# A bidirectional encoder layer: rsqrt of the input norm folded into retention, sums of squares taken tile by tile, the backward sweep in other PSUM banks

## The chip, the cores and the metric

The kernel runs on one core of a Trainium2 chip. The metric is the device time of one execution in microseconds; before the change it is 2090.89 us, the median of three runs from 2088.53 to 2091.76. TensorE makes the matmuls and transposes, VectorE (DVE), ScalarE (ACT) and GpSimd (POOL) work on elements, and SyncE (SP) issues every DMA of this kernel, in the order of its queue.

## The reference, cut to what matters

Two sequences, 512 and 1024 tokens of width 1024, pass one layer with the same weights: a token mixer (four heads of retention beside a gated MLP), cross-attention to a memory of 256 rows, and a SwiGLU. Each of the three has an RMS norm ahead of it and another behind it. The change touches the mixer.

```python
def rms_norm(x, w):
    y = x * rsqrt(mean(x * x, axis=-1) + EPS)
    return y * w
z = rms_norm(x, nw[NORM_PRE_MIX]) @ w_in
q, k, v, g, u, vs = split(z, ...)          # u, vs: the gated MLP; q, k, v, g: retention
q = rotary(q); k = rotary(k) * RET_HEAD_DIM ** -0.5
y = bidir_retention(q, k, v, log_gamma)    # chunks of 128 tokens, states carried both ways
ret_out = silu(g) * group_norm(y) * ret_gn_w
u = gelu(u); vs = layer_norm(gelu(vs), sgu_norm_w)
sgu_out = u * (sgu_w applied within a chunk to vs, + sgu_b)
mixed = concat(ret_out, sgu_out) @ w_out
```

In retention a chunk's scores q k^T are multiplied by a matrix of decays and applied to v; a forward state (sum of decayed k^T v) and a backward state add the other chunks.

## The kernel before, in words

The 1536 tokens are 12 tiles of 128. A float32 product is made of three matmuls (mm3, L149 to L151): both factors are split into a high part, written by ScalarE as fp32r (L135, or L139 with a scale), and the rest, written by VectorE (L136, L140). PSUM has eight banks of 128x512: four with the tag mm, four with the tag sm. A bank is given out again when its last reader is done.

*First stage.* z for u and vs of tiles 0 to 3 is accumulated in all eight banks (L214 to L231) while w_in is loaded. Then x_stats(0, 4) and x_stats(4, 8) (L293) load x tile by tile, ScalarE squares each and sums along the row (L245, L248), and after four tiles VectorE and GpSimd make rs_x = (mean + EPS)^-0.5 (L254, L163, L164). rs_x is then written to rsxd in HBM, transposed (L256), and read back as a row spread over all partitions (L257, rsx_row).

The loop over tiles 4 to 11 (L397) makes u and vs: 48 matmuls of 128x512 a tile (L409) into two mm banks. Between them run parts of generators: a tile's split for the next one (x_tile, L306), make_S, stats (x_stats(8, 12), then mem_stats for the memory's rows), and side, which holds post_uv of finished tiles: Gelu scaled by rs_x of the token, here a partition (L263, L264), layer norm (L266 to L272), two advances later the gating matmuls (L278), two later the transposes (L288) and a store to mixT (L291). make_S takes two tiles of x transposed, multiplies them by rsx_row (L316), forms four sums on GpSimd (L320 to L323), and stores seven left factors Sd (L326).

*z for retention.* q, k, v and g come from a scheme of seven products in place of eight for 2x2 blocks (z_units, 84 of 12 matmuls, mm bank each, L617 to L660): fetch_z loads a left factor (L352), split_z splits it, right_z makes the right factors. The results are added up in SBUF (c11 to c22).

*Retention.* While the z units run, point() (L581), called at most twice a unit, steps every generator in side once and starts a new tile of ret_feed at every second call. ret_tile is one head's chunk: rotary on GpSimd and VectorE (L472 to L477), transposes of q and k (L481, L482) into a bank pa, state products into a bank pb and the scores into pa (L492 to L503), the decays (L505), and in a next step the product with v (L507, L508, L510). ret_back goes over a sequence's chunks from the last to the first: a product with the backward state (L532), group norm, gate (L533 to L547), and one step later finish(): a transpose, a scaled copy (L522 to L524) and a store (L525). All of these banks have the tag sm.

The framework orders each engine's queue ahead of time by its own estimates; an engine works its queue in that order. Later stages (v and k of the memory, projections, attention, SwiGLU) are left as they are.

Of the kernel before, what the change touches and what calls it, by code (L numbers as in the profile page):

```python
# [17 lines left out]
P = 128  # L18
# [64 lines left out]
def encoder_kernel(ctx: ExitStack, tc, x, xTp, xTt, mem, memT, norm_w, w_in, lg, small, sgu_nw, sgu_wT,  # L83
# [23 lines left out]
    def sm():  # L107
        return psp.tile([P, 512], F32, tag="sm", name="sm")
# [89 lines left out]
    DT = [cB[:, 512 + h * P : 640 + h * P] for h in range(4)]  # L198
    swT = cC[:, 0:512]
    snB = cC[:, 512:1024]  # L200
    rsx_row = [sinT[:, 0:512], sinT[:, 512:D], cosT]
# [5 lines left out]
    Sd = {(n, j): dram.tile([P, 512], F32, tag=f"xs{n}_{j}", name=f"xs{n}_{j}") for n in range(1, 8) for j in range(6)}  # L207
    rsxd = dram.tile([NT, P], F32, tag="rsxd", name="rsxd")

    nc.sync.dma_start(sml, small)  # L210
    A.activation(rs_x, neg_half, AF.Copy)
# [20 lines left out]

    ss_x = const([P, NT], "ss_x")

    def squares(src, n, sums, done):

        q = deque()
        for t in n:
            r = raw.next()
            nc.sync.dma_start(r, src[t])  # L240
            q.append((t, r))
            if len(q) > 1:
                yield
                t, r = q.popleft()
                A.activation(r, r, AF.Square, accum_out=sums[:, t : t + 1])  # L245
        yield
        t, r = q.popleft()
        A.activation(r, r, AF.Square, accum_out=sums[:, t : t + 1])  # L248
        done()

    def x_stats(t0, t1):
        def done():
            s = slice(t0, t1)
            V.tensor_scalar_mul(ss_x[:, s], ss_x[:, s], 1.0 / D)  # L254
            rsqrt(rs_x[:, s], ss_x[:, s])
            nc.sync.dma_start(rsxd[t0:t1].rearrange("t p -> p t"), rs_x[:, s])  # L256
            nc.sync.dma_start(rsx_row[t0 // 4], rsxd[t0:t1].rearrange("t p -> (t p)").partition_broadcast(P))  # L257

        return squares(x, range(t0, t1), ss_x, done)

    def post_uv(t, pu, pv):
        u, vg = u_r.next(), vs_r.next()
# [27 lines left out]
        A.activation(m, pt, AF.Copy)  # L290
        nc.sync.dma_start(mixT[t][:, 4:8, :], m.rearrange("p (k t) -> p k t", t=P))  # L291

    for g in (x_stats(0, 4), x_stats(4, 8)):  # L293
        for _ in g:
            pass
    nc.sync.dma_start(swT, sgu_wT)
    nc.sync.dma_start(snB, sgu_nw.partition_broadcast(P))
    raw.slots, raw.i = FA.units[0:2], -1
# [11 lines left out]
        return o  # L310

    def make_S(j, xs):
        for t, r in zip((2 * j, 2 * j + 1), xs):
            r = r.rearrange("p (k t) -> p k t", t=P)
            row = rsx_row[t // 4][:, (t % 4) * P : (t % 4 + 1) * P]
            V.tensor_tensor(r, r, row.unsqueeze(1).broadcast_to([P, KT, P]), op=ALU.mult)  # L316
            yield
        a11, a12, a21, a22 = (r[:, i * 512 : (i + 1) * 512] for r in xs for i in range(2))
        s1, s2, s3, s4 = sums_x
        G.tensor_tensor(s1, a21, a22, op=ALU.add)  # L320
        G.tensor_tensor(s2, s1, a11, op=ALU.subtract)
        G.tensor_tensor(s3, a11, a21, op=ALU.subtract)
        G.tensor_tensor(s4, a12, s2, op=ALU.subtract)  # L323
        yield
        for n, src in ((1, a11), (2, a12), (4, a22), (5, s1), (6, s2), (7, s3), (3, s4)):
            nc.sync.dma_start(Sd[n, j], src)  # L326


# [1 line left out]
    rs_m = const([P, 4], "rs_m")  # L330

    def mem_stats():
        def done():
            V.tensor_scalar_mul(ss_m, ss_m, 1.0 / D)
            rsqrt(rs_m, ss_m)
            nc.sync.dma_start(rsd.rearrange("t p -> p t"), rs_m)

        return squares(mem, range(4), ss_m, done)

# [9 lines left out]
    def fetch_z(i):  # L349
        if i < len(z_units):  # L350
            Sq[i] = S_land.next()
            nc.sync.dma_start(Sq[i], Sd[z_units[i][1:]])  # L352

    def split_z(i):
        if i < len(z_units):
# [36 lines left out]
    for t in range(4):  # L392
        g = post_uv(t, *first[t])
        next(g)
        side.append(g)
    stats = x_stats(8, NT)
    for t in range(4, NT):  # L397
        a = nxt
        pss = [mm(), mm()]
        if t in (5, 8):  # L400
            x_load(0 if t == 5 else 2)
            x_load(1 if t == 5 else 3)
        j = {5: 2, 6: 0, 7: 3, 9: 4, 10: 1, 11: 5}.get(t)
        blocks = iter(()) if j is None else make_S(j, [xs.pop(2 * j), xs.pop(2 * j + 1)])
        for k in range(KT):
            ak = ksl(a, k)
            for x0, x1, st, sp in ((0, 0, True, False), (0, 1, False, False), (1, 0, False, True)):
                for i in range(2):
                    T.matmul(pss[i], lhsT=ak[x0], rhs=W[k][x1][:, i * 512 : i * 512 + 512],  # L409
                             start=st and k == 0, stop=sp and k == KT - 1)  # L410
            if k == 1 and t + 1 < NT:
                nxt = x_tile(t + 1)
            if t == NT - 1 and k % 2 == 0:
                right_z(1, 1, k // 2)
            if k % 2:
                next(blocks, None)
                next(stats, None)
            if k % 4 == 3 or t == 4 and k % 2:
                advance()
        g = post_uv(t, *pss)  # L420
        next(g)
        side.append(g)
        if t == 6:
            stats = mem_stats()
    RX = Part([RX.tiles[0], big("rx1", F32R), RX.tiles[2]])
    T_r.slots = T_r.slots + RX.units[7:9] + RX.units[3:5]
# [4 lines left out]


    dec = const([P, 6, 4], "dec")

    def decays():
        nc.sync.dma_start(cosT, cst[:, C_COS : C_COS + 512])
# [15 lines left out]
        A.activation(dec[:, 5, :], lgt[:, 4:8], AF.Exp, scale=float(P))  # L452
        V.tensor_scalar_mul(dec[:, 1:3, :], dec[:, 1:3, :], S_RET)

    ret = {}

    def ret_rings():
        ret["pk"] = carve(FC.units + FD.units, (512, 12))[0].slots
        names = "t1", "t2", "k", "kf", "st", "rf", "rb", "m"
        ret.update(zip(names, carve(FE.units, (256, 2), (256, 2), (P, 2), (2 * P, 2), (P, 1), (P, 1), (P, 2), (P, 2))))  # L460

    def ret_tile(h, c, n, t, z, pk, rf):
        ef, kfs, kbs, eb, gf, gb = (dec[:, i, h : h + 1] for i in range(6))
        yp, qT, wb, sg = pk
        A.activation(sg, z[:, 384:512], AF.Silu)

        t1, t2 = ret["t1"].next(), ret["t2"].next()
        zq = z[:, 0:256].rearrange("p (a s f) -> p s a f", a=2, s=2)
        t2q = t2.rearrange("p (a s f) -> p s a f", a=2, s=2)
        for s in range(2):  # L470
            o = c * P + s * 64
            G.tensor_tensor(t2q[:, s], zq[:, 1 - s],  # L472
                            sinT[:, o : o + 64].unsqueeze(1).broadcast_to([P, 2, 64]), op=ALU.mult)
        V.tensor_tensor(t1.rearrange("p (a f) -> p a f", f=64),
                        z[:, 0:256].rearrange("p (a f) -> p a f", f=64),
                        cosT[:, c * 64 : c * 64 + 64].unsqueeze(1).broadcast_to([P, 4, 64]), op=ALU.mult)
        V.tensor_tensor(t1, t1, t2, op=ALU.add)  # L477
        q, k, v = t1[:, 0:P], t1[:, P : 2 * P], z[:, 256:384]
        yield
        pa = sm()  # L480
        T.transpose(pa[:, 0:P], q, ident)  # L481
        T.transpose(pa[:, P : 2 * P], k, ident)  # L482
        kT = ret["k"].next()
        A.activation(qT, pa[:, 0:P], AF.Copy)
        A.activation(kT, pa[:, P : 2 * P], AF.Copy)
        kfb = ret["kf"].next()
        A.activation(kfb[:, 0:P], k, AF.Identity, scale=kfs)
        A.activation(kfb[:, P : 2 * P], k, AF.Identity, scale=kbs)
        yield
        pb = sm()  # L490
        if c > 0:
            T.matmul(pb[:, P : 2 * P], lhsT=kfb[:, P : 2 * P], rhs=v, start=True, stop=True)  # L492
        if c < n - 1:
            T.matmul(pb[:, 0:P], lhsT=kfb[:, 0:P], rhs=v, start=True, stop=True)
        if c > 0:
            T.matmul(pb[:, 256:384], lhsT=qT, rhs=rf, start=True, stop=True)
            A.activation(wb, pb[:, P : 2 * P], AF.Copy)
        if c < n - 1:
            if c == 0:
                V.tensor_copy(rf, pb[:, 0:P])  # L500
            else:
                V.scalar_tensor_tensor(rf, rf, gf, pb[:, 0:P], op0=ALU.mult, op1=ALU.add)
        T.matmul(pa[:, 256:384], lhsT=kT, rhs=qT, start=True, stop=True)  # L503
        sT = ret["st"].next()
        V.tensor_tensor(sT, pa[:, 256:384], DT[h], op=ALU.mult)  # L505
        yield
        T.matmul(pa[:, 384:512], lhsT=sT, rhs=v, start=True, stop=True)  # L507
        A.activation(yp, pa[:, 384:512], AF.Copy)  # L508
        if c > 0:
            V.scalar_tensor_tensor(yp, pb[:, 256:384], ef, yp, op0=ALU.mult, op1=ALU.add)  # L510

    def ret_back(h, t0, packs, tail):
# [5 lines left out]

        def finish():
            t, y = pend.popleft()  # L520
            pt = sm()
            T.transpose(pt[:, :P], y, ident)  # L522
            m = ret["m"].next()
            A.activation(m, pt[:, :P], AF.Identity, scale=sml[:, S_GN + h : S_GN + h + 1])  # L524
            nc.sync.dma_start(mixT[t][:, h, :], m)  # L525

        rb = None
        for c in range(n - 1, -1, -1):
            yp, qT, wb, sg = packs[c]
            if rb is not None:  # L530
                pb = sm()
                T.matmul(pb[:, 0:P], lhsT=qT, rhs=rb, start=True, stop=True)  # L532
                V.scalar_tensor_tensor(yp, pb[:, 0:P], eb, yp, op0=ALU.mult, op1=ALU.add)  # L533
            if c > 0:
# [918 lines left out]
```

## Time and profile before

| | |
|---|---|
| median of three runs | 2090.89 us (2088.53 to 2091.76) |
| profiled execution, its own time | 2092.05 us |
| its span in the profile | 2090.3 us |
| TensorE busy | 2016.9 us, 96% |
| VectorE, ScalarE, GpSimd busy | 60%, 46%, 36% |
| DMA, mean over the span | 149 GB/s |

The span runs from the first to the last instruction. A busy TensorE is one with a matmul in it; how fast this goes depends on the granted clock, which the profile gives as a share of full speed. An engine's waits name the instruction that came last.

### The profile page before, as it was taken

The numbers are of one execution on the slowest core, as the hardware profiler recorded it, in microseconds if no ns is written. First come the engines' busy times: TensorE is split into PE (matmuls) and PEld (weight loads), VectorE is DVE, ScalarE is ACT, GpSimd is POOL, SyncE is SP. The second block draws the span as 40 slices with busy tenths as digits, with TensorE's granted clock in tenths as the row PEclk, the third lists the DMA queues.
The fourth block names the chain that finished last, engine by engine and source line by source line (L and its number), as shares of the span: only waits on it lengthen the run. The fifth ranks groups of instructions, "written<-read, shape, count | busy, mean of one in ns | idle before, by whom it ended". The sixth has DMA issues, their size and how long they took to land. (4 is left out here: it accounts for less than half of the span.)

```text
span 2090.3 us, 29212 instructions
## 1 busy us (share of the span) xinstructions
PE 2016.9 (96%) x10298; PEld 1782.0 (85%) x10298; DVE 1248.4 (60%) x2163; ACT 961.1 (46%) x1967; POOL 744.1 (36%) x654
## 2 busy tenths in 40 slices
PE   8689999999999999999999999999999999999998
PEld 7467877778878888888888999999999999788887
DVE  3445687997743454453657666567656566845756
ACT  5433556666633443344445444445444444433332
POOL 0431104632313210001325667666766664000102
PEclk9889999999999999999999999999999999999999
DMA  8884464444362342233356543436343444845653
GB/s 230 208 241 163 124 190 123 122 138 148 119 211 91 131 141 71 71 107 116 129 168 202 155 134 115 128 104 193 115 125 106 125 128 138 281 159 198 214 186 132
DMA packets 186835, 312.49 MB, mean 149 GB/s; under 512 B 17728, under 2 KB 102080, under 8 KB 186688
## 3 DMA queue, kind: packets, MB, share of 16 engines
q1 hardware_dynamic: 186688, 310.62, 48.3%
q8 instruction: 81, 1.33, 0.3%
q14 instruction: 66, 0.54, 0.1%
HBM read 228.10 MB, written 82.45 MB: 149 GB/s over the span
## 5 line engine op out<-in xcount | busy, mean ns | idle before, releaser
L136 DVE TENSOR_TENSOR ra<-fa,ra 128x512 fp32r<-128x512 f32 (+1 forms) x168 | 166.6, 995 | 124.2 <-ACT ra L135 122.6
L135 ACT ACTIVATE ra<-fa 128x512 fp32r<-128x512 f32 (+1 forms) x168 | 107.1, 642 | 179.8 <-PE mm L150 148.0
L136 DVE TENSOR_TENSOR ra<-ra,ra 128x512 fp32r<-128x512 f32 x154 | 146.7, 953 | 53.6 <-ACT ra L135 53.2
L135 ACT ACTIVATE ra<-ra 128x512 fp32r<-128x512 f32 x154 | 97.2, 632 | 144.9 <-PE mm L150 141.4
L164 POOL TENSOR_TENSOR rs<-rq,neg_half 128x1 f32<-128x1 f32 x96 | 60.5, 631 | 277.7 <-DVE rq L163 267.5
L149 PE MATMUL mm<-rx,ra 128*128 128x384 f32 x440 | 148.2, 337 | 5.4 <-ACT rb L1194 3.1
L149 PE MATMUL mm<-rc,ra 128*128 128x384 f32 x440 | 147.8, 336 | 2.8 <-ACT rb L1194 2.8
L151 PE MATMUL mm<-rx,ra 128*128 128x384 f32 x440 | 147.8, 336 | 0.0
L150 PE MATMUL mm<-rx,ra 128*128 128x384 f32 x440 | 147.8, 336 | 0.0
L150 PE MATMUL mm<-rc,ra 128*128 128x384 f32 x440 | 147.4, 335 | 0.0
L151 PE MATMUL mm<-rc,ra 128*128 128x384 f32 x440 | 147.4, 335 | 0.0
L149 PE MATMUL mm<-rx,rc 128*128 128x512 f32 x288 | 116.4, 404 | 0.7 <-ACT rx L135 0.7
L150 PE MATMUL mm<-rx,rc 128*128 128x512 f32 x288 | 112.6, 391 | 0.6 <-DVE rx L136 0.6
L151 PE MATMUL mm<-rx,rc 128*128 128x512 f32 x288 | 112.8, 392 | 0.5 <-DVE rc L136 0.5
L1214 POOL TENSOR_TENSOR rb<-rb,rb 128x384 f32<-128x384 f32 x66 | 95.7, 1456 | 25.3 <-DVE rb L1202 18.5
L136 DVE TENSOR_TENSOR rx<-fa,rx 128x512 fp32r<-128x512 f32 (+1 forms) x67 | 63.8, 960 | 54.8 <-ACT rx L135 54.5
L135 ACT ACTIVATE rc<-fb 128x512 fp32r<-128x512 f32 (+2 forms) x56 | 52.4, 937 | 88.4 <-PE mm L150 67.7
L747 POOL TENSOR_TENSOR rx<-fa,rx 128x1024 fp32r<-128x1024 f32 x6 | 14.4, 2405 | 211.7 <-DMA fa<-oT 190.7
L149 PEld LDWEIGHTS mm<-rx,ra 128*128 128x128 f32 x440 | 83.1, 189 | 6.5 <-ACT rb L1194 3.8
L149 PEld LDWEIGHTS mm<-rc,ra 128*128 128x128 f32 x440 | 83.0, 189 | 3.8 <-ACT rb L1194 3.8
L150 PEld LDWEIGHTS mm<-rx,ra 128*128 128x128 f32 x440 | 83.2, 189 | 0.0
L151 PEld LDWEIGHTS mm<-rx,ra 128*128 128x128 f32 x440 | 83.2, 189 | 0.0
(535 smaller groups left out, 6065.2 us busy)
## 6 DMA issues: line engine op xcount, KB each, us to landing
hs<-rb SPq DMA_DIRECT2D x154, 192.0 KB, 2.4
fb<-hs SPq DMA_DIRECT2D x42, 704.0 KB, 4.2
fa<-in_wgu_dram SPq DMA_DIRECT2D x44, 512.0 KB, 4.0
ra<-in_wgu_dram SPq DMA_DIRECT2D x44, 512.0 KB, 3.6
rx<-in_wd_dram SPq DMA_DIRECT2D x77, 256.0 KB, 4.9
fa<-in_w_in_dram SPq DMA_DIRECT2D x66, 256.0 KB, 3.0
fb<-xs SPq DMA_DIRECT2D x48, 256.0 KB, 2.8
xs<-fd SPq DMA_DIRECT2D x24, 256.0 KB, 4.3
```

What stands on the lines that cost most here:

```text
L135: A.activation(hi, src, AF.Copy)
L136: V.tensor_tensor(lo, src, f32(hi), op=ALU.subtract)
L149: T.matmul(ps, lhsT=a[0], rhs=b[0], start=first, stop=False, skip_group_check=more)
L150: T.matmul(ps, lhsT=a[0], rhs=b[1], start=False, stop=False, skip_group_check=more)
L151: T.matmul(ps, lhsT=a[1], rhs=b[0], start=False, stop=last, skip_group_check=more)
L164: G.tensor_tensor(out, t, neg_half[:, :w], op=ALU.pow)
L747: G.tensor_tensor(a[1], r, f32(a[0]), op=ALU.subtract)
L1214: G.tensor_tensor(c[n], c[n], gated[n], op=ALU.mult)
```

## The change

x is no longer normalized before the retention products. In the scheme of seven products the left factors are made of plain x; four of them are stored, and the three that are blocks of x are read from the input. The factor rs_x is applied in ret_tile, where a token is a partition: to g in Silu, to q and k in the rotary, to the decays of the state products (dec_k, a new table of 12 tiles) and, for v, to the rows of the transposed scores. squares() takes its callback tile by tile: five tiles ahead of the loop, seven in it, and mem_stats starts one tile later. A ret_tile has one more step, between the decayed scores and the product with v, and other numbers of buffers. ret_back takes its two kinds of banks with the tag mm.

```diff
-    Sd = {(n, j): dram.tile(...) for n in range(1, 8) for j in range(6)}
-    rsxd = dram.tile([NT, P], F32, tag="rsxd", name="rsxd")
+    Sd = {(n, j): dram.tile(...) for n in (3, 5, 6, 7) for j in range(6)}
...
-    def squares(src, n, sums, done):
+    def squares(src, tiles, sums, done):
...
                 A.activation(r, r, AF.Square, accum_out=sums[:, t : t + 1])
+                done(t)
         yield
         t, r = q.popleft()
         A.activation(r, r, AF.Square, accum_out=sums[:, t : t + 1])
-        done()
-
-    def x_stats(t0, t1):
-        def done():
-            s = slice(t0, t1)
-            V.tensor_scalar_mul(ss_x[:, s], ss_x[:, s], 1.0 / D)
-            rsqrt(rs_x[:, s], ss_x[:, s])
-            nc.sync.dma_start(rsxd[t0:t1].rearrange("t p -> p t"), rs_x[:, s])
-            nc.sync.dma_start(rsx_row[t0 // 4], rsxd[t0:t1].rearrange("t p -> (t p)").partition_broadcast(P))
-
-        return squares(x, range(t0, t1), ss_x, done)
+        done(t)
+
+    def rs_of(t):
+        V.tensor_scalar_mul(ss_x[:, t : t + 1], ss_x[:, t : t + 1], 1.0 / D)
+        rsqrt(rs_x[:, t : t + 1], ss_x[:, t : t + 1])
...
-    for g in (x_stats(0, 4), x_stats(4, 8)):
-        for _ in g:
-            pass
+    for _ in squares(x, range(5), ss_x, rs_of):
+        pass
...
     def make_S(j, xs):
-        for t, r in zip((2 * j, 2 * j + 1), xs):
-            r = r.rearrange("p (k t) -> p k t", t=P)
-            row = rsx_row[t // 4][:, (t % 4) * P : (t % 4 + 1) * P]
-            V.tensor_tensor(r, r, row.unsqueeze(1).broadcast_to([P, KT, P]), op=ALU.mult)
-            yield
         a11, a12, a21, a22 = (r[:, i * 512 : (i + 1) * 512] for r in xs for i in range(2))
         s1, s2, s3, s4 = sums_x
+        yield
         G.tensor_tensor(s1, a21, a22, op=ALU.add)
+        G.tensor_tensor(s3, a11, a21, op=ALU.subtract)
+        yield
         G.tensor_tensor(s2, s1, a11, op=ALU.subtract)
-        G.tensor_tensor(s3, a11, a21, op=ALU.subtract)
         G.tensor_tensor(s4, a12, s2, op=ALU.subtract)
         yield
-        for n, src in ((1, a11), (2, a12), (4, a22), (5, s1), (6, s2), (7, s3), (3, s4)):
+        for n, src in ((5, s1), (6, s2), (7, s3), (3, s4)):
             nc.sync.dma_start(Sd[n, j], src)
...
-            nc.sync.dma_start(Sq[i], Sd[z_units[i][1:]])
+            _, n, j = z_units[i]
+            nc.sync.dma_start(Sq[i], {1: xTt[2 * j][:, 0:512], 2: xTt[2 * j][:, 512:D], 4: xTt[2 * j + 1][:, 512:D]}[n]
+                              if n in (1, 2, 4) else Sd[n, j])
...
-    stats = x_stats(8, NT)
+    stats = squares(x, range(5, NT), ss_x, rs_of)
...
-        if t == 6:
+        if t == 7:
             stats = mem_stats()
...
+        for t in range(NT):
+            V.tensor_scalar_mul(dec_k[:, t, :], dec[:, 1:3, :].rearrange("p a h -> p (a h)"), rs_x[:, t : t + 1])
...
-        ... (256, 2), (256, 2), (P, 2), (2 * P, 2), (P, 1), (P, 1), (P, 2), (P, 2)
+        ... (256, 2), (256, 1), (P, 3), (2 * P, 2), (P, 2), (P, 1), (P, 2), (P, 2)
...
-        ef, kfs, kbs, eb, gf, gb = (dec[:, i, h : h + 1] for i in range(6))
+        ef, gf, rs = dec[:, 0, h : h + 1], dec[:, 4, h : h + 1], rs_x[:, t : t + 1]
+        kfs, kbs = (dec_k[:, t, i * 4 + h : i * 4 + h + 1] for i in range(2))
-        A.activation(sg, z[:, 384:512], AF.Silu)
+        A.activation(sg, z[:, 384:512], AF.Silu, scale=rs)
...
-        V.tensor_tensor(t1..., z[:, 0:256]..., cosT..., op=ALU.mult)
-        V.tensor_tensor(t1, t1, t2, op=ALU.add)
+        V.scalar_tensor_tensor(t1..., z[:, 0:256]..., rs, cosT..., op0=ALU.mult, op1=ALU.mult)
+        V.scalar_tensor_tensor(t1, t2, rs, t1, op0=ALU.mult, op1=ALU.add)
...
-        V.tensor_tensor(sT, pa[:, 256:384], DT[h], op=ALU.mult)
+        V.scalar_tensor_tensor(sT, pa[:, 256:384], rs, DT[h], op0=ALU.mult, op1=ALU.mult)
+        yield
         yield
...
-            pt = sm()
+            pt = mm()
             T.transpose(pt[:, :P], y, ident)
...
-                pb = sm()
+                pb = mm()
                 T.matmul(pb[:, 0:P], lhsT=qT, rhs=rb, start=True, stop=True)
```

## Rows read from the trace of the kernel before

**Rows 1.** Page, part 1: busy time of each engine.

```profile
PE 2016.9 (96%) x10298; PEld 1782.0 (85%) x10298; DVE 1248.4 (60%) x2163; ACT 961.1 (46%) x1967; POOL 744.1 (36%) x654
```

**Rows 2.** TensorE's waits: us in total, times, longest.

```profile
PE mm L409 <- ACT fe L263: 16.3, 1, 16.3
PE sm L278 <- ACT fc L272: 8.2, 3, 4.1
PE sm L278 <- ACT fe L272: 7.6, 4, 4.1
...
PE sm L507 <- DVE fe L505: 5.1, 8, 0.9
PE sm L481 <- ACT fe L524: 3.5, 7, 1.2
```

**Rows 3.** Stretches: us, busy PE, PEld, DVE, ACT, POOL; PE clock, DMA share, GB/s.

```profile
51.60:68.10 16.50, 0.18 (x1) 0.00 (x0) 4.81 (x4) 5.37 (x8) 1.89 (x1) 0.58 0.69 177
68.10:196.60 128.50, 112.70 (x511) 93.13 (x512) 63.01 (x123) 47.68 (x78) 48.63 (x37) 0.92 0.76 216
...
290.00:600.00 310.00, 298.01 (x1597) 245.57 (x1596) 247.37 (x649) 191.71 (x551) 114.29 (x165) 1.00 0.48 143
...
440.00:470.00 30.00, 28.42 (x135) 21.83 (x134) 29.35 (x76) 20.53 (x51) 13.00 (x18) 1.00 0.49 141
```

**Rows 4.** Timeline of TensorE: start, us, instruction, [idle before <- releaser].

```profile
50.72 0.39 PE L151 MATMUL sm<-rb,rx 128*128 128x512 f32 x1
...
51.40 0.39 PE L151 MATMUL sm<-rb,rx 128*128 128x512 f32 x1
68.11 7.22 PE L409 MATMUL mm<-ra,rc 128*128 128x512 f32 x24 [16.32 <-ACT fe L263]
...
102.82 2.07 PE L278 MATMUL sm<-fe,fb 128*128 128x128 f32 x8 [4.14 <-ACT fe L272]
104.54 8.13 PE L409 MATMUL mm<-ra,rc 128*128 128x512 f32 x26
...
135.06 1.25 PE L278 MATMUL sm<-fc,fb 128*128 128x128 f32 x8 [4.08 <-ACT fc L272]
...
183.15 0.60 PE L288 MATMUL sm<-ident,fe 128*128 128x128 f32 x4
...
184.39 6.17 PE L409 MATMUL mm<-ra,rc 128*128 128x512 f32 x26
...
196.64 0.48 PE L149 MATMUL mm<-rx,rc 128*128 128x512 f32 x1
```

**Rows 5.** SyncE's own waits.

```profile
SPq L257 <- DMA rsxd<-rs_x: 27.0, 3, 11.2
```

**Rows 6.** Timeline of ScalarE.

```profile
22.15 1.06 ACT L245 ACTIVATE fa<-fa 128x1024 f32<-128x1024 f32 x1
...
64.91 1.06 ACT L245 ACTIVATE fa<-fa 128x1024 f32<-128x1024 f32 x1 [3.03 <-DMA fa<-in_x_dram]
...
67.37 2.42 ACT L263 ACTIVATE fe<-mm,rs_x 128x512 f32<-128x512 f32 x4
...
101.07 1.09 ACT L290 ACTIVATE fd<-sm 128x512 f32<-128x512 f32 x2 [11.19 <-DMA mixT<-fd]
```

**Rows 7.** Timelines of SyncE and ScalarE around the memory's rs write.

```profile
118.69 0.38 SPq L336 DMA_DIRECT2D rsd<-rs_m  x1
...
126.88 1.06 ACT L135 ACTIVATE rc<-rx 128x1024 fp32r<-128x1024 f32 x1 [8.45 <-DMA rx<-in_xTt_dram]
```

**Rows 8.** Timeline of GpSimd: the power -0.5 of four columns.

```profile
44.80 1.02 POOL L164 TENSOR_TENSOR rs_x<-rq,neg_half 128x4 f32<-128x4 f32 x1 [16.07 <-DVE rq L163]
```

**Rows 9.** VectorE's groups, 196.6 to 600 us, by form: count, busy us, mean ns.

```profile
L477 DVE TENSOR_TENSOR fe<-fe 128x256 f32<-128x256 f32 x48 | 21.0, 438 | 1.4
...
L140 DVE SCALAR_TENSOR_TENSOR rx<-fa,sml,rx 128x512 fp32r<-128x512 f32 x16 | 11.9, 755 | 3.4 <-ACT rx L139 3.4
...
L136 DVE TENSOR_TENSOR rc<-fe,rc 128x512 fp32r<-128x512 f32 x14 | 9.5, 680 | 6.2 <-ACT rc L135 6.2
```

More of the change, by code (lines that the diff above doesn't have):

```diff
@@ L200, in encoder_kernel @@
     snB = cC[:, 512:1024]
-    rsx_row = [sinT[:, 0:512], sinT[:, 512:D], cosT]
     W = [(RA.units + RB.units)[2 * k : 2 * k + 2] for k in range(KT)]
@@ L206, in encoder_kernel @@
     LEFTS = ("A11", "A12", "S4", "A22", "S1", "S2", "S3")
-    Sd = {(n, j): dram.tile([P, 512], F32, tag=f"xs{n}_{j}", name=f"xs{n}_{j}") for n in range(1, 8) for j in range(6)}
-    rsxd = dram.tile([NT, P], F32, tag="rsxd", name="rsxd")
+    Sd = {(n, j): dram.tile([P, 512], F32, tag=f"xs{n}_{j}", name=f"xs{n}_{j}") for n in (3, 5, 6, 7) for j in range(6)}
     nc.sync.dma_start(sml, small)
@@ L233, in encoder_kernel @@
     ss_x = const([P, NT], "ss_x")
-    def squares(src, n, sums, done):
+    def squares(src, tiles, sums, done):
         q = deque()
-        for t in n:
+        for t in tiles:
             r = raw.next()
@@ L332, in mem_stats, with done @@
     def mem_stats():
[L333 to L336, printed above, removed]
+        def done(t):
+            if t == 3:
+                V.tensor_scalar_mul(ss_m, ss_m, 1.0 / D)
+                rsqrt(rs_m, ss_m)
+                nc.sync.dma_start(rsd.rearrange("t p -> p t"), rs_m)
         return squares(mem, range(4), ss_m, done)
@@ L433, in encoder_kernel @@
     dec = const([P, 6, 4], "dec")
+    dec_k = const([P, NT, 8], "dec_k")
     def decays():
@@ L459, in ret_rings @@
         names = "t1", "t2", "k", "kf", "st", "rf", "rb", "m"
-        ret.update(zip(names, carve(FE.units, (256, 2), (256, 2), (P, 2), (2 * P, 2), (P, 1), (P, 1), (P, 2), (P, 2))))
+        ret.update(zip(names, carve(FE.units, (256, 2), (256, 1), (P, 3), (2 * P, 2), (P, 2), (P, 1), (P, 2), (P, 2))))
     def ret_tile(h, c, n, t, z, pk, rf):
-        ef, kfs, kbs, eb, gf, gb = (dec[:, i, h : h + 1] for i in range(6))
+        ef, gf, rs = dec[:, 0, h : h + 1], dec[:, 4, h : h + 1], rs_x[:, t : t + 1]
+        kfs, kbs = (dec_k[:, t, i * 4 + h : i * 4 + h + 1] for i in range(2))
         yp, qT, wb, sg = pk
-        A.activation(sg, z[:, 384:512], AF.Silu)
+        A.activation(sg, z[:, 384:512], AF.Silu, scale=rs)
         t1, t2 = ret["t1"].next(), ret["t2"].next()
@@ L473, in ret_tile @@
                             sinT[:, o : o + 64].unsqueeze(1).broadcast_to([P, 2, 64]), op=ALU.mult)
-        V.tensor_tensor(t1.rearrange("p (a f) -> p a f", f=64),
-                        z[:, 0:256].rearrange("p (a f) -> p a f", f=64),
-                        cosT[:, c * 64 : c * 64 + 64].unsqueeze(1).broadcast_to([P, 4, 64]), op=ALU.mult)
-        V.tensor_tensor(t1, t1, t2, op=ALU.add)
+        V.scalar_tensor_tensor(t1.rearrange("p (a f) -> p a f", f=64),
+                               z[:, 0:256].rearrange("p (a f) -> p a f", f=64), rs,
+                               cosT[:, c * 64 : c * 64 + 64].unsqueeze(1).broadcast_to([P, 4, 64]),
+                               op0=ALU.mult, op1=ALU.mult)
+        V.scalar_tensor_tensor(t1, t2, rs, t1, op0=ALU.mult, op1=ALU.add)
         q, k, v = t1[:, 0:P], t1[:, P : 2 * P], z[:, 256:384]
```

## The prediction

> **What bounds the kernel now.** I read the page's first part, then the list of TensorE's waits, then its stretches, then the timelines of the queues around the longest wait. TensorE is busy for 96% of the span [rows 1], so a gain can come only from the 73 us in which it stands, and from matmuls that run at a lowered clock. The waits say where [rows 2]: one of 16.3 us at L409, 15.8 us at L278, 8.6 us at L507 and L481. The first two lie between 51.6 and 196.6 us; the others in the retention stretch, 290 to 600 us.
>
> The stretches show the clock's part [rows 3]: the granted clock is 0.58 while TensorE stands at 51.6 to 68.1 us, 0.92 from there to 196.6 us, 1.00 later: a mix of the levels 1.2 and 2.4 GHz. What the first stage would take without stalls I work out from its timeline [rows 4]. Undisturbed 128x512 matmuls start (51.40 - 50.72)/3 = 0.227 us apart; tiles 4 to 11 have 8 x 48 = 384 of them, 87.2 us. One tile's transposes (L288) and gating matmuls (L278) take 184.39 - 183.15 = 1.24 us; the stretch holds ten and a half such pairs, 13.0 us. That makes 100.2 us. It runs from 51.63 to 196.64 us, 145.0 us. So **44.8 us** are lost there: 16.3 + 15.8 = 32.1 us of waits, and 12.7 us of slow matmuls after them (after the first wait 24 took 7.22 us in place of 24 x 0.227 = 5.45 us).
>
> **Why it stands.** SyncE spends 27.0 us in three waits for the write of rs_x to memory, up to 11.2 us each, ahead of the broadcast back [rows 5]. The write moves 512 single elements of 4 bytes (128 tokens of four tiles); whatever is issued behind it comes late. The loads of x tiles 8 and 9 stand behind the second one: the later of them is squared only at 64.91 us, and ScalarE has these squares in its queue ahead of the first Gelu, at 67.37 us [rows 6]. That Gelu frees the bank that L409 waits for.
>
> **The change, part by part.**
> 1. *rsxd write and broadcast removed, three times over.* The L409 wait loses its cause. Five tiles are squared before the loop, from 22.15 us on; a square takes 1.06 us, the power on GpSimd 1.02 us [rows 6, 8], so tiles 0 to 4 have their scale some 20 us before the first group of matmuls ends at 51.6 us. What is late next: Gelu of u for tiles 0 and 1, whose last matmuls stand 21 and 18 places from the end of that group, 4.8 and 4.1 us; then the chain Gelu, statistics, power, scaling for the gate, which has 24 matmuls, 5.4 us, as cover. I leave 1 us there. Gain 16.3 + (7.22 - 5.45) - 1.0 = **17.1 us**. Bounds: if ScalarE still has squares ahead of Gelu and their loads land as late as now, half stays (8 us gain); at most 18.1.
> 2. *Waits at the tile ends.* L278 waits for the scaled gate of the tile before. The stop of 4.14 us at 102.82 us follows the third such write: ScalarE waits 11.19 us for a store of mixT that stands behind it, with that scaling next in its queue [rows 4, 6]. The 26 matmuls after it take 8.13 us against 5.90; with 1 us on the gate itself, 7.4 us, which goes. The stop of 4.08 us at 135.06 us (some 6.2 us with its slow matmuls) follows the memory's own rsd write at 118.69 us, after which ScalarE waits 8.45 us for a tile [rows 4, 7]. That write **stays**, one tile later. Of the rest of the 44.8 us, 44.8 - 18.1 - 7.4 - 6.2 = 13.1 us, I take half: the twelve multiplications by rsx_row and 18 of 42 stores of 256 KB go, so GpSimd's sums start sooner, but all 24 stores that wait for those sums stay on SyncE's queue, ahead of later tile loads. Gain 7.4 + 6.5 = **14 us**; ends 0 and 26.7.
> 3. *Squares tile by tile.* Loads and squares of tiles 5 to 7 move into the tile loop, past Gelu on ScalarE and past tile loads on SyncE: 3 x 1.06 us on ScalarE. Twelve powers take the place of three (9 more on GpSimd, 9 us) with two small DVE operations each. All of this lies beside 12 us of TensorE work a tile; GpSimd was busy for 48.6 of 128.5 us [rows 3]. Cost 0; if that cover fails it is already the lower end of part 2. The left factors 1, 2 and 4 are now read from xTt in place of copies of it, in the same pieces: 0.
> 4. *Scaling folded into retention.* L474, L477 and L505 become the three-operand form. That form at 128x512 takes 755 ns against 680, 11% more; with L477's 438 ns for each of the three (L505 is half as wide) 3 x 0.438 x 0.11 = 0.14 us a tile, 48 tiles, 7 us of DVE [rows 9] over 310 us of which 247 are busy. Hidden, but in 440 to 470 us DVE is busy for 29.35 of 30 us [rows 3], where some of it may show: 0 to 1 us. The twelve small products for dec_k are far ahead of their use.
> 5. *One more step between scores and values.* L507 follows L505 by one step; with two the 5.1 us go [rows 2].
> 6. *Backward sweep in the mm banks.* The 3.5 us at L481 are a bank held by L524, a backward transpose; sm then serves the forward tiles alone. Against it: each forward tile holds its sm banks one step longer, and the main products share mm with 88 backward requests (48 transposes, 40 products). I charge 2 us, between 0 and the 8.6 us won. Gain of 5 and 6 together **6 us**, with 4 in it.
>
> The Trainium skill, "Vector Engine (DVE) Microarchitecture Reference", section "Points that are easy to get wrong", says that a scalar-tensor-tensor with two sources in SBUF that are not bf16 runs at half throughput. L140 [rows 9] is just that form with fp32 sources, and 11% slower, not 100%; by the page part 4 would cost 63 us of DVE in place of 7.
>
> **Sum.** 17.1 + 14 + 6 = 37 us. The profiled execution took 2092.05 us (span 2090.3); the median of the runs is 1.2 us lower. 2092.05 - 37 - 1.2 = 2054, and I say **2055**. The later stages stay bound by the same matmuls, so nothing gives it back.
>
> **The rivals.**
> *All the queues clear (17%).* With no 12 us blocks on the transfers the tile-end stops go too, but for 3 us: 41.8 + 8.6 = 50 us, **2041**. For it: three of the four blocking writes go. Against: the fourth stays, and so do the stores that wait for sums.
> *Stops change their names only (18%).* Part 1 holds; the tile ends wait for loads as before, and new bank waits eat part 6: **2074**. For it: transfers are busy for 0.76 of the stage [rows 3], and a shorter stage moves nearly the same bytes.
> *The change doesn't do what it says (2%).* Squares of tiles 5 to 8 stay ahead of Gelu and wait for their two landing places: half of the first stop stays; with the rest as forecast 2055 + 9 = **2064**.
> *Half-rate vector operations (2%).* The DVE gets up to 48 x 3 x 0.438 = 63 us more, in a stretch that has 310 - 247 = 63 us of room but is full in places; if half of it shows, 2055 + 32 = **2087**, no change that can be told. Rows 9 speak against it. The page cited above speaks for it.
> *Slower (3%).* The main products wait for mm banks held by the backward sweep. The longest L481 wait was 1.2 us [rows 2]; 88 requests at that price are 105 us, **2160**. It decides from 36/88 = 0.41 us a request; slower by 0.2% from 0.45. Against it: a bank of either kind is held for a small part of the time between two steps, and main products use two of the four.
>
> **How the numbers follow.** The forecast has 58%, with an own range of 2044 to 2066. To leave out no more than 2 in 10 the range takes in the larger parts of the two next cases: **2038 to 2076**. A measurement of this kernel tells some 0.2%, 4 us, from no change. Faster by more: forecast, clear queues, renamed stops, half stop, 0.95. Within 0.2%: half rate, 0.02. Slower: 0.03.
>
> **What would show it.** Right: no wait of L409 over 2 us near 52 us; the first matmul of the z products (196.64 us now) at 160 to 172 us; no wait of L507; L278 stops of 4 to 9 us in sum, one of them behind L336. Wrong: L409 waiting still for a Gelu with a square ahead of it; waits at L149 in the retention stretch that end with L533 or L524 (banks); L474 near 0.8 us (half rate). If the z products start before 157 us the queues cleared; after 180 us the stops were renamed.

## The result, and the profile after

The changed kernel takes **2063.51 us** (median of four runs, 2060.81 to 2065.07) against 2090.25 us of the kernel before beside it: a ratio of 0.9871, 95% interval 0.9854 to 0.9888. That is 26.7 us off the median, where 36 were forecast; the time lies inside the range, 8.5 us above the predicted 2055. The profiled execution is the fastest of the four (2060.81 us, span 2059.0), while the one before (2092.05 us) was a long one, so the two spans differ by 31.3 us.

I aligned the two traces at three matmuls: the first of the z products (196.64 us before [rows 4], 174.61 us after), the one six matmuls ahead of retention's first transpose of q (307.37 and 282.83), and the first of the projections (615.32 and 588.03). The page's first part and TensorE's waits (us in total, times, longest) of the kernel after:

```profile
PE 2008.3 (98%) x10298; PEld 1778.7 (86%) x10298; DVE 1252.0 (61%) x2181; ACT 962.1 (47%) x1967; POOL 745.7 (36%) x663
```

```profile
PE sm L271 <- ACT fc L265: 7.8, 2, 6.1
...
PE sm L281 <- DVE fe L274: 5.5, 1, 5.5
PE sm L494 <- ACT fd L482: 2.4, 4, 1.2
PE mm L521 <- ACT fd L546: 2.2, 6, 0.6
PE mm L521 <- ACT fc L546: 1.7, 3, 0.9
PE sm L271 <- ACT fe L265: 1.3, 1, 1.3
...
PE sm L501 <- ACT fe L483: 1.2, 1, 1.2
...
PE mm L531 <- ACT rx L135: 1.1, 1, 1.1
```

Lines have moved: L401 is L409 of before, L271 is L278, L281 is L288, L265 is L272, L503 is L505, L506 is L507, L494 is L496, L521 is L522 and L531 is L532. Beside [rows 2], the 16.3 us at L409, the 5.1 us at L507 and the 3.5 us at L481 are gone; of the 15.8 us at L278 9.1 stay, and L281 has a stop that is new. The waits at L494, L521, L501 and L531 lie in retention and have grown or are new.

The same three stretches of both kernels (us; busy PE, PEld, DVE, ACT, POOL; clock, DMA share, GB/s): the tile loop, the z products alone, retention. Before:

```profile
51.60:196.64 145.04, 112.92 (x513) 93.17 (x513) 67.82 (x127) 53.09 (x85) 50.52 (x37) 0.88 0.75 211
196.64:307.37 110.73, 108.95 (x488) 89.46 (x486) 76.30 (x131) 60.33 (x126) 15.17 (x15) 1.00 0.50 149
307.37:615.32 307.95, 294.69 (x1582) 242.47 (x1580) 240.97 (x634) 184.87 (x531) 113.40 (x163) 1.00 0.47 143
```

After:

```profile
51.60:174.61 123.01, 108.44 (x518) 90.94 (x517) 52.29 (x121) 46.03 (x76) 41.43 (x39) 0.93 0.59 174
174.61:282.83 108.22, 108.22 (x487) 89.53 (x486) 78.67 (x145) 61.25 (x126) 16.24 (x13) 1.00 0.51 153
282.83:588.03 305.20, 292.88 (x1581) 241.83 (x1580) 248.55 (x632) 185.97 (x531) 117.76 (x165) 1.00 0.48 146
```

The first stage gave 145.0 - 123.0 = **22.0 us** (31 forecast), the z products 110.73 - 108.22 = **2.5** (nothing forecast), retention 307.95 - 305.20 = **2.75** (6 forecast), the rest up to the span's end 1475.0 - 1471.0 = 4.0. No part of the change lies in the rest, and in the kernels below, which have the same code there, it takes 1470.7 to 1477.5 us, so I leave it out. The z products take 108.1 to 110.8 us in the kernels below; no run shows what makes the difference. With the pure work of 100.2 us that the prediction worked out, the first stage still loses 22.8 us: 14.6 us of waits and 8.2 more, of which 1.0 is that the first group of matmuls ends at 52.61 in place of 51.63 us, and the rest lies mainly in slow matmuls behind the stops. The forecast left 44.8 - 31.1 = 13.7. TensorE's timeline shows where:

```profile
52.61 5.60 PE L401 MATMUL mm<-ra,rc 128*128 128x512 f32 x24
60.38 1.16 PE L271 MATMUL sm<-fe,fb 128*128 128x128 f32 x8 [1.28 <-ACT fe L265]
63.25 3.56 PE L271 MATMUL sm<-fc,fb 128*128 128x128 f32 x16 [1.71 <-ACT fc L265]
114.44 1.25 PE L281 MATMUL sm<-ident,fe 128*128 128x128 f32 x4 [5.47 <-DVE fe L274]
121.80 2.07 PE L271 MATMUL sm<-fc,fb 128*128 128x128 f32 x8 [6.11 <-ACT fc L265]
123.53 8.23 PE L401 MATMUL mm<-ra,rc 128*128 128x512 f32 x26
174.61 0.48 PE L149 MATMUL mm<-rx,rc 128*128 128x512 f32 x1
```

The tile loop's first group of matmuls (L401) now starts at once. Two stops of 5.47 and 6.11 us remain at 109 to 122 us, and behind them 26 matmuls take 8.23 us in place of 5.90; from 123.5 to 126.5 us the granted clock is 0.50. Timelines of SyncE, ScalarE and VectorE show the chain that leads there, and last of all comes one of SyncE's own waits:

```profile
96.70 0.38 SPq L326 DMA_DIRECT2D rsd<-rs_m  x1
99.15 1.23 SPq L360 DMA_DIRECT2D fa<-in_w_in_dram  x2
111.82 0.72 ACT L369 ACTIVATE fa<-fa,sml 128x512 f32<-128x512 f32 x1 [15.37 <-DMA fa<-in_w_in_dram]
113.11 0.67 ACT L256 ACTIVATE fe<-mm,rs_x 128x512 f32<-128x512 f32 x1
113.23 0.89 DVE L136 TENSOR_TENSOR rx<-fa,rx 128x512 fp32r<-128x512 f32 x1 [19.20 <-ACT rx L135]
```

```profile
SPq L326 <- POOL rs_m L164: 8.0, 1, 8.0
```

At 96.70 us the memory's rs row is written to rsd, 512 single elements, as rs_x was before. Loads of w_in for the first z products are issued behind it; ScalarE has the scaling of that block (L369), with which its split begins, in its queue ahead of the Gelu of a finished tile (L256), and stands for 15.37 us, VectorE for 19.20. SyncE had also waited 8.0 us for rs_m before it could issue the write, and the loads behind it waited with it. Before, three writes of rs_x and this one came in turn; this one is left, and it now reaches TensorE twice. The transfers in 90 to 115 us, in 40 equal slices (share of the 16 DMA engines in tenths, GB/s), and the write's time to landing:

```profile
DMA  9998410000004999190000940323227999791829
GB/s 393 423 420 334 190 52 0 0 0 0 0 0 3 380 239 13 10 13 0 0 0 3 16 10 3 10 10 26 20 20 233 406 406 406 295 380 36 331 89 347
...
rsd<-rs_m SPq DMA_DIRECT2D x1, 2.0 KB, 12.5
```

From the 16th slice to the 30th (99.4 to 108.8 us) hardly a byte moves, 0 to 26 GB/s, and the DMA engines are shown mostly idle, although loads of w_in have been issued at 99.15 us. (The zeros in slices 7 to 12 are SyncE's wait for rs_m, in which it issued nothing.) It takes 12.5 us until the 2 KB have landed.

### The profile page after: what moved, and what is told of

It reads as the page before. It is cut to its first block, busy times and chain, and to the rows that moved or that the text cites. A ratio compares the mean times of both kernels' runs of the same rounds, so it can differ in the third digit from the quotient of the medians.

```text
span 2059.0 us, 29195 instructions
## 1 busy us (share of the span) xinstructions
PE 2008.3 (98%) x10298; PEld 1778.7 (86%) x10298; DVE 1252.0 (61%) x2181; ACT 962.1 (47%) x1967; POOL 745.7 (36%) x663
## 5 line engine op out<-in xcount | busy, mean ns | idle before, releaser
L136 DVE TENSOR_TENSOR ra<-ra,ra 128x512 fp32r<-128x512 f32 x154 | 151.3, 984 | 52.7 <-ACT ra L135 52.3
L164 POOL TENSOR_TENSOR rs<-rq,neg_half 128x1 f32<-128x1 f32 x96 | 59.8, 624 | 270.5 <-DVE rq L163 262.3
L149 PE MATMUL mm<-rc,ra 128*128 128x384 f32 x440 | 148.2, 337 | 3.8 <-ACT rb L1193 3.8
L149 PE MATMUL mm<-rx,ra 128*128 128x384 f32 x440 | 148.0, 336 | 3.2 <-ACT rb L1193 2.2
L149 PE MATMUL mm<-rx,rc 128*128 128x512 f32 x288 | 116.3, 404 | 0.0
L1213 POOL TENSOR_TENSOR rb<-rb,rb 128x384 f32<-128x384 f32 x66 | 95.2, 1448 | 25.2 <-DVE rb L1201 18.9
L149 PEld LDWEIGHTS mm<-rc,ra 128*128 128x128 f32 x440 | 83.1, 189 | 4.8 <-ACT rb L1193 4.7
L149 PEld LDWEIGHTS mm<-rx,ra 128*128 128x128 f32 x440 | 83.2, 189 | 4.0 <-ACT rb L1193 2.5
L150 PEld LDWEIGHTS mm<-rc,ra 128*128 128x128 f32 x440 | 83.2, 189 | 0.0
L151 PEld LDWEIGHTS mm<-rc,ra 128*128 128x128 f32 x440 | 83.2, 189 | 0.0
```

The lines of the kernel that those rows point to most:

```text
L136: V.tensor_tensor(lo, src, f32(hi), op=ALU.subtract)
L149: T.matmul(ps, lhsT=a[0], rhs=b[0], start=first, stop=False, skip_group_check=more)
L150: T.matmul(ps, lhsT=a[0], rhs=b[1], start=False, stop=False, skip_group_check=more)
L151: T.matmul(ps, lhsT=a[1], rhs=b[0], start=False, stop=last, skip_group_check=more)
L164: G.tensor_tensor(out, t, neg_half[:, :w], op=ALU.pow)
L1213: G.tensor_tensor(c[n], c[n], gated[n], op=ALU.mult)
```

## The experiments

My theory after the result: in the first stage the change gains only by not writing 512 single elements (three of four such writes go), and the fourth holds back what is missing of the forecast; in retention the extra step and the mm banks gain, not the folding. Rivals: fewer multiplications and stores in the first stage; transfers as a whole; a part of the retention change by itself; folding itself. Where the z products start (z), and how long it is from there to the first projection (418.7 us before, 615.32 - 196.64; 413.4 after), tells the two halves apart. The 412.2 us of some expectations ends at 586.80 us, 1.2 ahead of the first projection. Each of these is read from one trace: z of kernels with the same first stage differs by 0.5 us (174.1 to 174.6) in one case and by 3.4 (193.19 and 196.64) in another. Ratios are to the kernel before, run beside each.

**The memory's row by TensorE.** From the changed kernel: a transpose of rs_m to a row (four advances after it is made) and a write of four pieces of 512 bytes.

```diff
-                nc.sync.dma_start(rsd.rearrange("t p -> p t"), rs_m)
+        pt = sm()
+        T.transpose(pt[0:4, 0:P], rs_m, ident)
+        A.activation(row, pt[0:4, 0:P], AF.Copy)
+        nc.sync.dma_start(rsd, row)
```

> The changed kernel, but rs_m becomes a row by a transpose on TensorE and is stored in four pieces of 512 B; the write of 512 single elements is gone. Theory (the stops of 5.5 and 6.1 us at 114 and 122 us come from this write, which holds up the w_in loads behind it): both stops go with the slow matmuls after them, first matmul of the z products at 158 to 163 us in place of 174.6, time 11 to 16 us below the changed kernel, about 2049. Rival (the stops come from the order of the queues, w_in loads ahead of Gelu on ScalarE, and from SyncE's stores that wait for sums): the stops stay within 3 us, time 2060 to 2064.

2050.7 us, ratio 0.9825 (0.9806 to 0.9843); z at 163.96 us. TensorE's waits of this kernel's first stage:

```profile
PE sm L271 <- ACT fc L265: 5.0, 2, 3.3
...
PE sm L271 <- ACT fe L265: 1.1, 1, 1.1
```

```profile
112.28 1.16 PE L271 MATMUL sm<-fc,fb 128*128 128x128 f32 x8 [3.32 <-ACT fc L265]
```

Of the two long stops the one at L281 is gone and the one at L271 is down from 6.11 to 3.32 us: 14.6 us of waits became 6.1, and z starts 174.61 - 163.96 = 10.7 us sooner, with 163.96 just above the 158 to 163 expected. The row is now stored at 157.72 us, so this run takes away both the single elements and SyncE's wait for rs_m ahead of the loads; the 10.7 us are for both together. By the medians this kernel takes 12.8 us less than the changed one, by the ratios 0.46%, 9.6 us.

**Three dead writes.** The changed kernel, with rs_x still written in single elements as before, three times, and never read.

```diff
+        if t % 4 == 3:
+            nc.sync.dma_start(rsxd[t - 3 : t + 1].rearrange("t p -> p t"), rs_x[:, t - 3 : t + 1])
```

> The changed kernel with the three writes of rs_x to rsxd put back, transposed, 512 single elements each, which nobody reads. Theory (the element writes made the stalls of the first stage of the kernel before): most of the stage's gain of 22 us is lost, z products from 186 us on or later, time 2075 or more. Rival (the twelve multiplications, the broadcasts and the 18 stores made them): the stage keeps its length within 4 us, time 2062 to 2068.

2082.43 us, ratio 0.9973 (0.9962 to 0.9984), z at 195.92. TensorE's waits:

```profile
PE sm L275 <- ACT fc L269: 10.7, 3, 6.4
PE sm L285 <- DVE fe L278: 9.9, 1, 9.9
...
PE sm L275 <- ACT fe L269: 5.7, 2, 3.8
PE mm L405 <- ACT fe L260: 4.0, 2, 2.1
```

ScalarE and VectorE meanwhile, on their timelines:

```profile
111.05 1.06 ACT L245 ACTIVATE fa<-fa 128x1024 f32<-128x1024 f32 x1 [13.62 <-DMA fa<-in_mem_dram]
113.18 1.22 DVE L136 TENSOR_TENSOR rc<-fc,rc 128x1024 fp32r<-128x1024 f32 x1 [27.55 <-DMA rx<-in_xTt_dram]
```

Nobody reads what is written, yet 195.92 - 174.61 = 21.3 of the 22.0 us are lost again, though at other places: the stops at L405 (L409 of before) are 4.0 us where one was 16.3, and those at the tile ends are 26.3. TensorE waits for ScalarE and VectorE, and these up to 13.62 and 27.55 us for loads of the memory's rows and of x, which have nothing to do with it. So it is the writes, not the wait for the broadcast that followed them. This run does not separate the single elements from SyncE's waits for rs_x ahead of the writes (17.0 us in three); the next one does.

**Before, with the write in memory's own order.** The same bytes as 128 pieces of 16; the row then has its values in the wrong places.

```diff
-            nc.sync.dma_start(rsxd[t0:t1].rearrange("t p -> p t"), rs_x[:, s])
+            nc.sync.dma_start(rsxd[t0:t1].rearrange("t p -> (t p)").rearrange("(p t) -> p t", t=4), rs_x[:, s])
```

> The kernel before with the write to rsxd in the order in which the partitions hold it, 128 pieces of 16 B in place of 512 of 4 B; the values then stand in wrong places of rsx_row, all else (waits, broadcast, multiplications, stores) stays. Theory (number of elements in the write): the wait for the write falls from 9 us to 3 to 4, the L409 stop from 16.3 to under 6 us, time 12 to 20 us below before. Rival (round trip, broadcast and multiplications cost the time, not the elements): L409 stop over 12 us, time within 6 us of before.

2063.15 us, ratio 0.9878 (0.9862 to 0.9895), 24.2 us below before where 12 to 20 were expected; no wait at L409 is left; z at 170.71, from there 418.6 us. The DMA issues of the kernel before, and below them those of this one (KB each, median us to landing):

```profile
rsxd<-rs_x SPq DMA_DIRECT2D x3, 2.0 KB, 12.5
rsd<-rs_m SPq DMA_DIRECT2D x1, 2.0 KB, 10.6
```

```profile
rsxd<-rs_x SPq DMA_DIRECT2D x3, 2.0 KB, 1.8
rsd<-rs_m SPq DMA_DIRECT2D x1, 2.0 KB, 10.5
```

SyncE's waits around these writes in this kernel:

```profile
SPq L256 <- POOL rs_x L164: 19.7, 3, 7.9
SPq L257 <- DMA rsxd<-rs_x: 1.8, 2, 1.3
```

SyncE still stands for rs_x ahead of the three writes (18.9 us before), so those waits are not what cost the time. The same 2 KB land after 1.8 us in place of 12.5, and one line alone gives as much as the whole change; the first stage is 3.9 us shorter than the change's, with all multiplications and stores still in it.

**The retention part alone.** The kernel before with the extra step, the buffers and the mm banks.

```diff
+        yield
...
-            pt = sm()
+            pt = mm()
...
-                pb = sm()
+                pb = mm()
```

> The kernel before with only the retention part of the order: one more step before the product with v, the numbers of buffers, the backward sweep in mm banks; no folding. Theory (prediction's parts 5 and 6): no L507 wait left, stretch from z to the projection 5 to 6 us shorter, time 2084 to 2086. Rival (new waits on banks and on ScalarE take the place of the old): within 2 us of before.

2083.09 us, ratio 0.9976 (0.9967 to 0.9986); 609.16 - 193.19 = 416.0 us from z to the projections, 2.7 less than before, half of what was expected. The waits for the decayed scores are gone but for 0.4 us.

**One of the two undone.** From the changed kernel, first without the extra step (the second `yield` taken out), then with the backward sweep in sm.

> The changed kernel without the extra step between the decayed scores and the product with v; the backward sweep stays in the mm banks. If the extra step is what shortens retention: 48 waits for the decayed scores come back (5 us or more of L507's kind), time 2066 to 2069, the stretch from the first z product to the projection 4 to 6 us longer than the changed kernel's 412.2 us. If the banks are what shortens it: within 2 us.

> The changed kernel with the backward sweep in the sm banks again; the extra step stays. If the banks matter: each forward tile holds its banks a step longer now, so waits for sm banks at the transposes of q and k come back and grow, over 4 us in sum (3.5 in the kernel before), the stretch 4 us longer or more. If they do not: the stretch within 2 us of 412.2.

Without the step: 2069.21 us, ratio 0.9909 (0.9892 to 0.9926); 421.3 us from z. In sm: 2068.02 us, ratio 0.9908 (0.9893 to 0.9924); 421.0 us. Their waits, each kernel in turn:

```profile
PE sm L505 <- DVE fe L503: 8.8, 10, 2.6
```

```profile
PE sm L531 <- ACT fe L523: 4.9, 4, 1.9
PE sm L479 <- ACT fe L523: 4.0, 4, 1.7
```

Both expectations named the right waits, with stretches 7.6 to 7.9 us longer than the changed kernel's, more than the 4 to 6 expected without the step. Without the step the product with v (L505 in that kernel) waits for its scores; in sm the transposes of q (L479) and the backward product (L531) wait for banks. What each of the two gains by itself is seen only beside the kernel that has neither, which follows.

**Neither: folding alone in retention.** Step, buffers and banks as before; rs_x still folded.

> The changed kernel with the retention stage's numbers of buffers, steps and banks as before: no extra step, backward sweep in sm, rs_x still folded into retention's own operations. Theory (in retention folding saves nothing and costs a little VectorE time; only the extra step and the mm banks together gain): z products at 174 to 175 us, the stretch from there to the projections 418 to 422 us (before 418.7), the waits for the decayed scores (5 us or more) and at the transposes of q (about 3.5 us) back, time 2066 to 2071 us. Rival (folding itself brings part of the 5.3 us of this stretch): 413 to 416 us there, time 2064 us or less.

2070.88 us, ratio 0.9918 (0.9902 to 0.9935); 597.87 - 174.07 = 423.8 us, 1.8 above the upper end of what was expected and 5.1 more than before. The wait for the decayed scores is back:

```profile
PE sm L505 <- DVE fe L503: 6.4, 10, 2.6
```

Retention alone, from the matmul six ahead of its first transpose of q to the first projection, in all kernels here:

| rs_x | step, banks | kernels | us |
|---|---|---|---|
| ahead of the products | neither | before, and the two with other row writes | 307.2 to 308.5 |
| ahead of the products | both | retention part alone; cheap rows with it | 305.1; 302.5 |
| folded | neither | this one | 315.7 |
| folded | banks only | without the step | 312.9 |
| folded | step only | backward sweep in sm | 311.8 |
| folded | both | the changed kernel and four others | 304.2 to 305.5 |

Folding by itself costs retention 315.7 - 307.95 = 7.7 us, where kernels with the same retention code differ by 1.3 to 2.7. With rs_x folded, the banks alone gain 2.8 us, the step alone 3.9, and both 10.5, more than their sum; with rs_x ahead, both gain 2.8 in one pair of kernels and 4.75 in the other.

**Folding left out, the rows cheap.** The kernel before, with all its multiplications and stores and its values in place; only the four rows are turned on VectorE and written in pieces of 128 bytes. Then the same with the retention part.

```diff
+        V.tensor_copy(wide[:, 0:4], rs)
+        V.transpose(tr, wide)
+        for b in range(4):
+            nc.sync.dma_start(dst[:, b * 32 : b * 32 + 32], tr[b * 32 : b * 32 + 4, :])
```

> The kernel before, still with x normalized ahead of the products, its twelve multiplications and all its stores; only the three rows of rs_x and the memory's rs row are turned on VectorE (32x32 transposes) and written as four pieces of 4 rows x 128 bytes in place of 512 single elements. Theory (in the first stage the change gains only by writing no single elements; folding the norm is worth nothing there): no L409 wait over 2 us, the z products start at 160 to 171 us, the stretch from there to the projections stays at 418.7 us as before, time 2054 to 2063 us. Rival (the multiplications and the 18 stores that folding removes are worth something once the queues are clear): z products at 172 us or later, time 2066 us or more.

> The kernel of the run before this one (x still normalized ahead, rows written in pieces of 128 bytes) with the change's extra step, buffers and mm banks for the backward sweep. Theory (the parts add; folding the norm into retention is itself worth nothing): z products at 160 to 171 us, 413 to 416 us from there to the projections, time 2050 to 2059 us, level with the changed kernel whose memory row goes by TensorE (2050.7). Rival (folding is worth something in retention, where the step alone gave 2.7 us and the whole change 5.3, or in the first stage): 6 us or more above that kernel, 2057 us or more; or the retention part gives nothing here.

First: 2057.25 us, ratio 0.9866 (0.9849 to 0.9882), level with the whole change; z at 165.42, then 417.1 us. Second: 2051.26 us, ratio 0.9836 (0.9817 to 0.9856), level with the best kernel above; z at 165.84, then 411.9. So folding, which gives the change its name, is worth nothing that shows once the writes are cheap: z at 165.4 and 165.8 against 163.96 us, 411.9 against 412.9 us behind it. The first of the two also prices the memory's write near its old place: against the kernel above that still wrote it in single elements, z comes 170.71 - 165.42 = 5.3 us sooner, with all other rows cheap in both, against the scatter of up to 3.4 above. The transfers in 28 to 53 us, where the first two rows are written, of the kernel before and below it of the first of these two:

```profile
DMA packets 1889, 2.25 MB, mean 90 GB/s; under 512 B 1148, under 2 KB 1148, under 8 KB 1889
```

```profile
DMA packets 2012, 6.05 MB, mean 242 GB/s; under 512 B 285, under 2 KB 285, under 8 KB 2010
```

In the same 25 us 2.7 times the bytes move, with a quarter of the small packets.

**Two attempts on the rest.** Both start from the kernel with the memory's row by TensorE. One gates tiles 2 and 3 a step later, since two short stops at 60 to 66 us remain; the other issues make_S's stores on GpSimd's queue.

```diff
-            if k % 4 == 3 or t == 4 and k % 2:
+            if t == 4 and k == 3:
+                for g in side[:2]:
+                    next(g)
+            elif k % 4 == 3 or t == 4 and k % 2:
```

> As e1_mem_row_by_pe, and in tile 4 the gating matmuls of tiles 2 and 3 one step later than those of 0 and 1. Theory (the waits of 1.1 and 1.7 us at 60 and 63 us are the chain Gelu, statistics, power, scaling of four tiles in a row): both waits under 0.5 us, z products 3 to 4 us earlier than 164.0, time 2 to 4 us below e1. Rival (the chain is late by the sums on GpSimd and comes late anyway): no change within 1 us.

```diff
-            nc.sync.dma_start(Sd[n, j], src)
+            nc.gpsimd.dma_start(Sd[n, j], src)
```

> As e1_mem_row_by_pe, with make_S's 24 stores issued from GpSimd's queue behind its sums in place of SyncE's. Theory (the stop of 3.3 us at 112 us comes from w_in loads that stand behind stores on SyncE): the w_in loads go out before 95 us, the stop goes, time 3 to 6 us below e1. Rival (GpSimd pays for the issues, and its powers for Gelu's chain come later): stops at the tile ends grow, time above e1.

Staggered: 2052.69 us, ratio 0.9832 (0.9815 to 0.985), z 0.9 us sooner, no gain: one of the two waits went, the other stayed at 1.13 us. On GpSimd: 2062.18 us, ratio 0.9881 (0.9866 to 0.9895), z at 172.89, 8.9 us later. The w_in loads did go out at 83 to 90 us and the stop of 3.3 us went, as its theory said, but stops of 5.58 us at 59 and of 7.22 at 100 us came. Its wait and GpSimd's timeline:

```profile
PE sm L271 <- ACT fe L265: 12.8, 2, 7.2
```

```profile
63.09 0.55 POOL L164 TENSOR_TENSOR rs<-rq,neg_half 128x1 f32<-128x1 f32 x1
...
64.20 0.57 POOL L164 TENSOR_TENSOR rs<-rq,neg_half 128x1 f32<-128x1 f32 x1
...
65.95 1.12 POOL L315 DMA_DIRECT2D xs<-fd  x2
67.09 0.56 POOL L164 TENSOR_TENSOR rs<-rq,neg_half 128x1 f32<-128x1 f32 x1
```

GpSimd makes the powers of the layer norm (L164) that the gates wait for; with stores and sums between them they come 1 to 3 us apart. In the changed kernel the sums alone stand among them; that is probably where its 3.0 us at 60 to 63 us come from, but no run took them away.

## Why the prediction was right, and where it was not

*Right in what bounded the kernel and in direction.* Of the signs named, the L409 wait is gone, L507's wait is gone, no wait of L149 ends with L532 or L523 (L533 and L524 of before), and one of the L271 stops lies behind the write of rsd. The z products start at 174.61 us, outside the 160 to 172 named. L271's stops, 9.1 us, and L281's 5.5 are more than the 4 to 9.

*Step 1, the removed writes: right.* The stop at L409 goes as soon as the writes are cheap, with the squares in their old order. Its 17.1 us left 1 us on the gate chain; the stops there are 1.28 + 1.71 = 3.0 us, a term too small by 2.

*Step 2 failed in its size:* "That write stays, one tile later", priced at 6.2 us, its cost before. In the changed kernel the stops behind it cost more: 5.47 + 6.11 us and 8.23 - 5.90 = 2.3 us of slow matmuls in one group make 13.9, and taking the write out of the stage gave 10.7. In the kernel before the loads behind it were those of a tile [rows 7]; moved a tile on, it has loads of w_in behind it whose split ScalarE has queued ahead of a Gelu, so that both the transpose and the gate of a tile wait. The prediction looked at what the write had cost, not at what stands behind it in its new place. How much of the 10.7 us is the single elements and how much SyncE's wait of 8.0 us for rs_m no run separates; near its old place the elements were worth 5.3 us. The half of the remaining 13.1 us that it booked to fewer multiplications and stores had the wrong cause: those are worth nothing that shows here.

*Step 3, squares tile by tile: 0 forecast, and nothing shows it otherwise.* The z products start at 163.96 us with them and at 165.42 without, both with cheap rows. With three dead writes the stops at the first group were 4.0 us in place of 16.3, so with fewer squares ahead of Gelu slow writes may cost less there; no run shows it by itself.

*Step 4, folding: hidden, as forecast, only together with steps 5 and 6.* VectorE's groups of the changed kernel, 174 to 590 us, that answer to L477 and L505 (count, busy us, mean ns, idle before):

```profile
L475 DVE SCALAR_TENSOR_TENSOR fe<-fe,rs_x 128x256 f32<-128x256 f32 x48 | 25.8, 538 | 3.4 <-POOL fe L469 1.2
...
L503 DVE SCALAR_TENSOR_TENSOR fe<-sm,rs_x,fb 128x128 f32<-128x128 f32 x48 | 16.2, 338 | 0.6 <-PE sm L501 0.6
```

L475 takes 538 ns against 438 [rows 9], 23% more, and L503 338 against 279 for L505 before, 21%; 48 of each add 7.6 us. L471, for L474 before, adds 1.0 (25.1 against 24.1), so all three add 8.6 where 7 were forecast. By the rule of the Trainium skill ("Vector Engine (DVE) Microarchitecture Reference", "Points that are easy to get wrong") L475, two fp32 sources in SBUF, would have taken twice 438, an estimate of 876 ns; the trace does not agree. But "0 to 1 us" on the path held by the cover of steps 5 and 6 alone: without them folding cost retention 7.7 us.

*Steps 5 and 6 failed in their size; that the sum looks right is luck.* From z to the projections 5.3 us were gained for 6 forecast, but 2.5 of them lie ahead of retention's first tile, where nothing was forecast; retention gave 2.75. Both named waits went, 8.6 us, but the charge of 2 us for new ones was too small: TensorE's waits that the profile lists in retention, without that of the first projection, are 11.0 us before and 11.1 after. They now lie at products that want copies of q and k from ScalarE (L494, L501) and at the backward sweep's transposes and products (L521, L531). The two were also booked as separate gains, and with rs_x folded they are worth 2.8 and 3.9 us alone, 10.5 together, of which 7.7 pay for folding.

*The rivals.* "Stops change their names only" came nearest in part: a stop at the tile ends has a new releaser, and new waits ate half of the retention gain, though the time was 10 us below its 2074. "All queues clear" is what the kernel with the memory's row by TensorE shows, but for 6 us of waits: 2050.7, where the rival said 2041. Neither a bank wait of the main products nor half-rate vector operations came.

*What stays open.* The 2.5 us in the z products; why step and banks together gain more than each by itself; and why with rs_x ahead they gave 2.8 us in one pair and 4.75 in the other.

## What to carry to other kernels

Look for transfers of single elements in a stage full of loads: their own size says nothing, and what they cost falls on whatever is queued behind them, on work that never reads them. Turn such a row on an engine first and write it in long pieces; and price a write that is moved by its new neighbours, not by what it cost in the old place. Where two edits gain little each, measure them together too, beside a kernel with neither, align traces at the same matmul and not at the same time, and test a change of algorithm against the plain repair of what it happens to remove.

## What the runs showed of the hardware

A write of 512 elements of 4 bytes from SBUF to HBM landed after 9.9 to 12.6 us in these runs; the same 2 KB in 128 pieces of 16 bytes landed after 1.4 to 2.7 us, 1.8 in the median. What the other transfers did meanwhile was not always the same. For 9 us behind the memory's write of the changed kernel they moved 0 to 26 GB/s. But behind that of the kernel before (118.69 us, landed after 10.6) they went on, at 270 to 407 GB/s for 3 to 4 us and then at 56 to 170; its transfers in 115 to 140 us, in 40 slices:

```profile
GB/s 400 400 374 341 393 295 341 393 407 284 270 301 98 79 75 125 170 69 56 92 92 72 59 170 406 410 387 383 387 351 216 295 7 26 0 0 331 380 128 121
```

Why transfers slow down or stand still behind such a write is not shown by these traces. The Trainium skill ("DMA: Bandwidth & Descriptors", "Why small descriptors are slow") charges each piece a fixed overhead. By that a quarter of the pieces would cost a quarter, an estimate; the landing went down to a seventh, and a stop of other transfers is not in that rule.

A wait that is too short to show can probably still cost: matmuls of 128x512 start 0.227 us apart but are drawn 0.39 us long [rows 4], so gaps up to 0.16 us look busy. Between the same two matmuls the idle time of retention fell by 307.95 - 294.69 - (305.20 - 292.88) = 0.9 us, the stretch by 2.75.
